# Seven block products in place of eight in part of w_down of a hybrid decoder layer

## The chip, the cores and the metric

The kernel runs on one core of one Trainium2 chip. TensorE (PE) multiplies, VectorE (DVE), ScalarE (ACT) and GpSimd (POOL) work on tiles in SBUF, the first two also read the results of TensorE in PSUM, and SyncE (SP) issues nearly all DMAs. The metric is the device time of one execution in microseconds (us), as a median over runs.

## The reference

One decoder layer in float32 on x of 256 tokens by 2048 columns: attention in two groups of heads, then an MLP with gates. Each of the two is wrapped as x + norm(f(norm(x))). The attention and its projections are not touched by the change; the second half is:

```python
h = rmsnorm(x, pre_ffn_g[l])
u = causal_dwconv(h @ w_up[l], conv_w[l], conv_b[l])
gate, val = jnp.split(u, 2, axis=-1)
y = (jax.nn.gelu(gate, approximate=True) * val) @ w_down[l]
x = x + rmsnorm(y, post_ffn_g[l])
```

w_up is 2048 by 11264, w_down is 5632 by 2048 (44 row blocks of 128). Each weight is read from memory once in a run.

## The kernel before

**Numbers.** A float32 operand is split into a high part (hi, a rounded copy that ScalarE writes) and the rest (lo, a subtraction on VectorE), `w_split` for weights (L106) and `split` for activations (L285). A product is three matmuls, hi by hi, hi by lo and lo by hi (`mm3`, L279).

**Weights.** `w_load` (L69) has SP load a unit of 128 by 1024 numbers (512 KB) into one of five `raw` buffers; `w_split` writes its parts to one of five `whi` and five `wlo` buffers (`w_parts`, `WB`). A raw buffer comes free after the subtraction, a whi or wlo buffer after the last matmul that reads it.

**Order of the work.** TensorE's instructions run in the order in which the code is written. From the first group of the MLP (`order.__exit__`) until the last `manual_schedule` near L1010 the other engines' order is made by a planner, by priority (place in the code) and by when operands and buffers are ready. Buffers of a tag are handed out by it too. Each engine executes its queue in order.

**The MLP.** The 5632 hidden columns are worked in two halves of 22 blocks (`FHALF`). A half has 11 groups of two blocks: TensorE computes 256 columns of gates and 256 of values (`proj_T`), `conv` (L849) adds the two parts of the result (L853, L854), scales (GpSimd, L855) and applies the convolution (ScalarE L857, VectorE L859, L861); gate and value are multiplied (L930) and split into G (hi and lo, both 128-token blocks t side by side).

Then comes w_down for that half: for each block of 512 output columns n, two PSUM banks (t = 0 and 1) take 11 units of two row blocks, 12 matmuls a unit. `down` (L943) takes a bank to y_sb: in half 0 a copy on ScalarE, in half 1 an addition on VectorE, a sum of squares on ScalarE and a multiplication by the norm's gain on GpSimd (L951). In half 1 the last 512 columns go otherwise: rows of t = 0 in `b0`; rows of t = 1 in two banks `b1` of 256 columns each, for the first five units (`LAST`) beside `b0`, for the last six (`HOLD`) after it, from parts that are kept (`held`; two units of them in `rest`). `finish` (L990) multiplies by the norm's factor, adds x_sb and sends the result out.

**Memory.** PSUM has four banks with the tag "acc" and four with "att"; the groups of the up-projection take them in turn (`alt`). x_sb (256 by 2048, tag "x") stays in SBUF from the end of the attention until `finish`.

## Time and profile before

| | us |
|---|---|
| time, median of 3 runs (1067.03 to 1067.55) | 1067.05 |
| profiled execution, its own time | 1067.17 |
| its span, first to last instruction | 1065.3 |
| TensorE's clock in it, as granted | 0.998 |
| up-projection of half 1, stage window 695.80 to 936.70 | 240.9 |
| w_down of half 0, 576.00 to 696.00 | 120.0 |
| w_down of half 1, 936.70 to 1057.30 | 120.6 |
| from there to the end | 8.0 |

The stage windows give, for a stretch of the span, the busy time of each engine with its count of instructions in brackets, then the granted clock, the share of the DMA engines and GB/s. A group of instructions reads: line, engine, operation, tile written<-tiles read, shapes, count, then busy time in us and mean ns of one, then the engine's idle time just before them and which instruction ended it. A timeline reads: start, length, engine, line, operation, count. In all of them matmuls are pipelined, so that the record of one overlaps the next.

### The profile page before, as it was taken

Reading aid. Unit: us, or ns where it says so; the run is one execution under the profiler, and the core shown is the slowest. Engines: PE = TensorE matmul, PEld = TensorE weight load, DVE = VectorE, ACT = ScalarE, POOL = GpSimd, SP = SyncE. Lnnn points to the kernel's source line nnn. Section 1 sums busy time; section 2 is a strip of 40 time slices with the busy share of each in tenths; the row PEclk is TensorE's granted clock in tenths of the full one; section 3 lists DMA queues with packets and bytes.
Section 4 is the critical chain, followed back from the end, with each engine's and each line's share of the span. In section 5 each row is a group of like instructions: output and inputs, shape, how many; then the busy total and the mean of one; then the engine's idle time right before and its main releaser. Section 6 shows DMA issues by size and latency. Waiting matters only on the chain.

```text
span 1065.3 us, 16215 instructions
## 1 busy us (share of the span) xinstructions
PE 1055.4 (99%) x5974; PEld 919.2 (86%) x5974; DVE 738.3 (69%) x1200; ACT 614.0 (58%) x1062; POOL 226.2 (21%) x250
## 2 busy tenths in 40 slices
PE   9999999999999999999999999999999999999997
PEld 7889988888889888888888888888888888888886
DVE  5989868886568877777677444457777777755563
ACT  6776757767548655556565443456565555644450
POOL 4353245440122312112121000002121212201110
PEclk9999999999999999999999999999999999999999
DMA  8645667545863766566666666666666666666642
GB/s 290 191 127 175 181 191 213 176 153 160 296 223 122 236 197 193 183 198 197 197 187 185 202 196 195 194 186 198 183 199 192 195 181 198 197 195 194 192 170 79
DMA packets 164970, 202.88 MB, mean 190 GB/s; under 512 B 6780, under 2 KB 130972, under 8 KB 164380
## 3 DMA queue, kind: packets, MB, share of 16 engines
q1 hardware_dynamic: 164572, 201.45, 61.2%
q8 instruction: 47, 0.77, 0.3%
q10 hardware_dynamic: 320, 0.40, 0.1%
q14 instruction: 31, 0.25, 0.1%
HBM read 199.58 MB, written 2.11 MB: 189 GB/s over the span
## 4 chain that ended last, share of the span: by engine, by line
PE 94%; DVE 2%; issue 1%; DMA 1%; ACT 1%; POOL 1%; SPq 0%; DVEq 0%; POOLq 0%; ACTq 0%
PE bank_acc L283 34%; PE bank_acc L261 22%; PE bank_att L261 14%; PE bank_acc L268 11%; PE bank_att L268 7%; PE bank_att L449 1%; PE bank_att L484 1%; PE bank_att L493 1%; DVE wlo L120 1%; PE bank_acc L879 1%; PE bank_att L283 1%; DMA x_in<-in_x_dram 1%; PE bank_att L495 0%; PE bank_att L732 0%; POOL scr L416 0%
## 5 line engine op out<-in xcount | busy, mean ns | idle before, releaser
L120 DVE TENSOR_TENSOR wlo<-raw,whi 128x1024 fp32r<-128x1024 f32 (+3 forms) x357 | 435.7, 1230 | 239.1 <-ACT whi L117 232.7
L117 ACT CAST whi<-raw 128x1024 fp32r<-128x1024 f32 (+3 forms) x356 | 363.3, 1035 | 269.2 <-issue 121.2
L261 PE MATMUL bank_acc<-hT,whi 128*128 128x512 f32 x1088 | 260.6, 391 | 0.0
L261 PEld LDWEIGHTS bank_acc<-hT,whi 128*128 128x128 f32 x1088 | 200.1, 188 | 39.5
L283 PE MATMUL bank_acc<-whi,G 128*128 128x512 f32 x652 | 202.7, 389 | 0.0
L855 POOL TENSOR_TENSOR u<-u,rowf 128x256 f32<-128x256 f32 x88 | 96.6, 1118 | 493.5 <-DVE u L854 490.6
L261 PE MATMUL bank_att<-hT,whi 128*128 128x512 f32 x640 | 150.6, 390 | 0.0
L283 PEld LDWEIGHTS bank_acc<-whi,G 128*128 128x128 f32 x652 | 122.4, 188 | 25.0
L261 PEld LDWEIGHTS bank_att<-hT,whi 128*128 128x128 f32 x640 | 118.7, 188 | 23.9
L268 PEld LDWEIGHTS bank_acc<-hT,wlo 128*128 128x128 f32 x1088 | 131.1, 188 | 3.3
L268 PE MATMUL bank_acc<-hT,wlo 128*128 128x256 f32 x1088 | 133.4, 278 | 0.0
L283 PE MATMUL bank_acc<-wlo,G 128*128 128x512 f32 x326 | 126.9, 389 | 0.0
L283 PE MATMUL bank_acc<-whi,oT 128*128 128x512 f32 (+1 forms) x272 | 81.7, 379 | 0.0
L268 PEld LDWEIGHTS bank_att<-hT,wlo 128*128 128x128 f32 x640 | 76.0, 188 | 1.7
L268 PE MATMUL bank_att<-hT,wlo 128*128 128x256 f32 x640 | 76.3, 277 | 0.0
L283 PEld LDWEIGHTS bank_acc<-wlo,G 128*128 128x128 f32 x326 | 61.2, 188 | 12.3
L283 PEld LDWEIGHTS bank_acc<-whi,oT 128*128 128x128 f32 x272 | 50.2, 188 | 9.3
L283 PE MATMUL bank_acc<-wlo,oT 128*128 128x512 f32 (+1 forms) x136 | 51.2, 377 | 0.0
L283 PE MATMUL bank_acc<-whi,hT 128*128 128x384 f32 (+1 forms) x192 | 46.9, 323 | 0.0
L857 ACT ACTIVATE yg<-u,cw 128x256 f32<-128x256 f32 x44 | 26.5, 602 | 27.5 <-POOL u L855 27.5
L857 ACT ACTIVATE yv<-u,cw 128x256 f32<-128x256 f32 x44 | 26.4, 603 | 26.5 <-POOL u L855 26.5
L416 POOL TENSOR_TENSOR scr<-scr 128x256 f32<-128x256 f32 x26 | 26.7, 1042 | 57.2 <-DVE scr L415 34.3
(212 smaller groups left out, 1056.5 us busy)
## 6 DMA issues: line engine op xcount, KB each, us to landing
raw<-in_w_up_dram SPq DMA_DIRECT2D x176, 512.0 KB, 4.1
raw<-in_w_down_dram SPq DMA_DIRECT2D x88, 512.0 KB, 4.7
raw<-in_w_in_dram SPq DMA_DIRECT2D x51, 512.0 KB, 4.7
raw<-in_w_out_dram SPq DMA_DIRECT2D x32, 512.0 KB, 4.7
raw<-in_w_in_dram SPq DMA_DIRECT2D x16, 384.0 KB, 3.3
cb<-c_dram SPq DMA_DIRECT2D x8, 256.0 KB, 4.3
x_sb<-in_x_dram SPq DMA_DIRECT2D x2, 1024.0 KB, 5.9
raw<-in_w_in_dram SPq DMA_DIRECT2D x5, 408.0 KB, 4.1
```

Source lines behind the costliest of these rows:

```text
L117: i1 = act.copy(hi[:, cs], raw[:, cs])
L120: i2 = dve.tensor_tensor(lo[:, cs], raw[:, cs], hi[:, cs].bitcast(F32), op=ALU.subtract)
L261: pe.matmul(b, hi[:, a, m * P:(m + 1) * P], hT[:, kt, 0:512], start=(kt == 0), stop=(last == (0, kt)))
L268: pe.matmul(b[:, 256:512], lo[:, a, m * P:(m + 1) * P], hT[:, u * 4 + a, 0:256], start=False, stop=(last == (1, u * 4 + a)))
L283: pe.matmul(b, a, r[:, cols], start=(first and i == 0), stop=(last and i == 2))
L416: pool.tensor_tensor(dst, dst, row, op=ALU.mult)
L449: pe.matmul(sb[e][:, cs], a[r, t * P:(t + 1) * P], b[r, 0:nk], start=(n == 0), stop=(n == 2))
L484: pe.transpose(pb[:, i * P:(i + 1) * P], p[:, e, c:c + P], ident)
L493: pe.matmul(ov, values(hl, 0), p[:, :, 0:256], start=(n == 0), stop=False)
L855: pool.tensor_tensor(u[:, 2:258], u[:, 2:258], rowf, op=ALU.mult)
L857: act.activation(y, u[:, 2:258], AF.Identity, bias=cw[:, 3, ch:ch + 1], scale=cw[:, 2, ch:ch + 1])
L879: pe.matmul(v(b, t), gate[kt][0][:, ms], v(hT[:, kt, 0:512], t), start=(t == 0 and kt == 0), stop=False)
```

## The change

Of the 11 pairs of row blocks of a half, the first five (`WIN`) are multiplied in Strassen's way, in Winograd's form. With A the two blocks of activations of 128 tokens by two row blocks, and B two row blocks by two column blocks of 512 (two loads, `left` and `right`), eight block products become seven. Three of them are over A11, A12 and A22 themselves, one over S1 = A21+A22 (which takes A21's place in G), three over S2, S3 and S4, which are made once in the up-projection by four sums on GpSimd and kept, split, in `sums`. On the side of the weights four sums of 128 by 512 (T1 to T4) are made on GpSimd for each seven, in place in the raw buffers, after B11, B22 and B21 have been split, and then split themselves.

Each pair of column blocks (n, n+1) now takes all eight banks: b, e, g, h collect the four results directly, and a, c, d, f the four products that several results share. `fold` adds these to y_sb after the fifth seven, on VectorE, and in half 1 on GpSimd too. A round is: three products of a seven, one pair of row blocks in the old way for n (`four`) and one for n+1, then the other four products. There are five such rounds and one without a seven. In half 1 the second column pair has no bank h: its old-way products of n+1 come afterwards, for t = 0 in e and for t = 1 as before in `b1`.

`sums` needs the memory of x_sb: x is written to DRAM in the first group and read back near the end (`x_dram`, `x_end`). In half 1 the four gain multiplications of columns 0 to 1023 are collected (`later_on`) and run after the last fold, and the parity of `alt` is turned round.

```diff
+WIN = 5
...
+        x_dram = tc.dram_tile([2 * P, D], F32, name="x_dram")
...
+            if half:
+                sums = main.tile([P, WIN, 768], F32R, tag="x", name="sums")
             for g in range(FHALF // 2):
                 c0 = (half * (FHALF // 2) + g) * 256
-                alt = g % 2
+                alt = (g + half) % 2
...
+                ys = []
                 for m in range(2):
                     y = conv(bv[m], 44 + c0 // P + m, "yv")
                     dve.tensor_tensor(y, y, gates[m], op=ALU.mult)
+                    ys.append(y)
+                if g < WIN:
+                    if half == 0 and g == 0:
+                        for t in range(2):
+                            sp.dma_start(x_dram[t * P:(t + 1) * P, :], x_sb[:, t, :])
+                        sums = main.tile([P, WIN, 768], F32R, tag="x", name="sums")
+                    s = fp.tile([P, 512], F32, tag="s", name="s")
+                    (a11, a21), (a12, a22) = [(y[:, 0:P], y[:, P:256]) for y in ys]
+                    pool.tensor_tensor(s[:, P:256], a11, a21, op=ALU.subtract)
+                    pool.tensor_tensor(a21, a21, a22, op=ALU.add)
+                    pool.tensor_tensor(s[:, 0:P], a21, a11, op=ALU.subtract)
+                    pool.tensor_tensor(s[:, 256:384], a12, s[:, 0:P], op=ALU.subtract)
+                for m, y in enumerate(ys):
                     gt = G[g * 2 + m]
                     split(gt[:, 0:256], gt[:, 256:512], y)
+                if g < WIN:
+                    split(sums[:, g, 0:384], sums[:, g, 384:768], s[:, 0:384])
...
-                b1 = [bank("att"), bank("att")]
-                for b, cs in zip(b1, halves):
-                    pe.matmul(b[:, cs], G[0][:, 0:P], G[0][:, 0:256], start=True, stop=False)
-                    act.copy(b[:, cs], y_sb[:, 1, 1536:2048][:, cs])
-            def down(t, n, b):
+            gains = []
+            def down(t, n, b, gain=None):
                 ys = y_sb[:, t, n * 512:(n + 1) * 512]
-                if half == 0:
-                    act.copy(ys, b)
-                else:
-                    dve.tensor_tensor(ys, b, ys, op=ALU.add)
+                dve.tensor_tensor(ys, b, ys, op=ALU.add)
+                if half:
                     act.activation(junk, ys, AF.Square, scale=D ** -0.5,
                                    accum_out=ysq[t][:, n:n + 1])
-                    pool.tensor_tensor(ys, ys, gbf[:, n * 512:(n + 1) * 512], op=ALU.mult)
+                    (gain or pool.tensor_tensor)(ys, ys, gbf[:, n * 512:(n + 1) * 512], op=ALU.mult)
             LAST = FHALF // 2 - HOLD
-            for n in range(3 + (half == 0)):
-                b2 = [bank(), bank()]
-                for u in range(FHALF // 2):
-                    hi, lo = w_unit(w_rows(w_down, half * FHALF + u * 2, 2, n * 512, 512), 2, 512)
-                    for a in range(2):
-                        k = u * 2 + a
-                        for t in range(2):
-                            mm3(b2[t], G[k], t, hi[:, a, :], lo[:, a, :], slice(0, 512), k == 0,
-                                k == FHALF - 1)
-                for t in range(2):
-                    down(t, n, b2[t])
+            def products(b, held, hi, lo, opened, closes=False):
+                for i, (x, r) in enumerate(((held[0], hi), (held[0], lo), (held[1], hi))):
+                    pe.matmul(b, x, r, start=b not in opened and not i,
+                              stop=closes and i == 2)
+                opened.append(b)
+            def parts_of(k, t):
+                return G[k][:, t * P:(t + 1) * P], G[k][:, 256 + t * P:256 + (t + 1) * P]
+            def split_512(dst, i, src):
+                cs = slice(i * 512, i * 512 + 512)
+                hi, lo = dst[0][:, cs], dst[1][:, cs]
+                split(hi, lo, src)
+                return hi, lo
+            def seven(n, u, banks, opened):
+                b, e, g, a, c, d, f = banks
+                k = half * FHALF + u * 2
+                left, right = [w_load(w_rows(w_down, k, 2, m * 512, 512), 2, 512)[0]
+                               for m in (n, n + 1)]
+                b11, b21, b12, b22 = (x[:, i * 512:i * 512 + 512] for x in (left, right)
+                                      for i in range(2))
+                s2, s3, s4 = [(sums[:, u, i * P:i * P + P], sums[:, u, 384 + i * P:512 + i * P])
+                              for i in range(3)]
+                dst = w_parts(UNIT, held=False)
+                w11 = split_512(dst, 0, b11)
+                w22 = split_512(dst, 1, b22)
+                w21 = split_512(w_parts(UNIT, held=False), 0, b21)
+                pool.tensor_tensor(b11, b12, b11, op=ALU.subtract)
+                pool.tensor_tensor(b12, b22, b12, op=ALU.subtract)
+                pool.tensor_tensor(b22, b22, b11, op=ALU.subtract)
+                pool.tensor_tensor(b21, b21, b22, op=ALU.subtract)
+                last = u == WIN - 1
+                products(a, parts_of(u * 2, 0), *w11, opened, last)
+                products(b, parts_of(u * 2 + 1, 0), *w21, opened)
+                products(e, s4, *w22, opened)
+                def others():
+                    dst = w_parts(UNIT, held=False)
+                    t1 = split_512(dst, 0, b11)
+                    t3 = split_512(dst, 1, b12)
+                    dst = w_parts(UNIT, held=False)
+                    t2 = split_512(dst, 0, b22)
+                    t4 = split_512(dst, 1, b21)
+                    products(d, parts_of(u * 2, 1), *t1, opened, last)
+                    products(f, s3, *t3, opened, last)
+                    products(c, s2, *t2, opened, last)
+                    products(g, parts_of(u * 2 + 1, 1), *t4, opened)
+                return others
+            def four(n, u, pair, opened):
+                hi, lo = w_unit(w_rows(w_down, half * FHALF + u * 2, 2, n * 512, 512), 2, 512)
+                for i in range(2):
+                    for t in range(2):
+                        products(pair[t], parts_of(u * 2 + i, t), hi[:, i, :], lo[:, i, :], opened,
+                                 u == FHALF // 2 - 1 and i == 1)
+            def fold(n, a, c, d, f):
+                y11, y12, y21, y22 = (y_sb[:, t, m * 512:(m + 1) * 512] for t in range(2)
+                                      for m in (n, n + 1))
+                if half == 0:
+                    act.copy(y11, a)
+                    dve.tensor_tensor(y22, c, y11, op=ALU.add)
+                    dve.tensor_tensor(y12, d, y22, op=ALU.add)
+                    dve.tensor_tensor(y21, f, y22, op=ALU.add)
+                    dve.tensor_tensor(y22, d, y21, op=ALU.add)
+                else:
+                    s = fp.tile([P, 512], F32, tag="s", name="s")
+                    act.copy(s, a)
+                    dve.tensor_tensor(y11, a, y11, op=ALU.add)
+                    dve.tensor_tensor(s, c, s, op=ALU.add)
+                    pool.tensor_tensor(y12, y12, s, op=ALU.add)
+                    dve.tensor_tensor(y12, d, y12, op=ALU.add)
+                    dve.tensor_tensor(s, f, s, op=ALU.add)
+                    pool.tensor_tensor(y21, y21, s, op=ALU.add)
+                    dve.tensor_tensor(s, d, s, op=ALU.add)
+                    pool.tensor_tensor(y22, y22, s, op=ALU.add)
+            for n in (0, 2):
+                opened = []
+                tail = half and n
+                shared = [bank("att") for _ in range(4)]
+                b, e, g = [bank() for _ in range(3)]
+                h = None if tail else bank()
+                for i in range(FHALF // 2 - WIN):
+                    others = i < WIN and seven(n, i, (b, e, g, *shared), opened)
+                    four(n, WIN + i, (b, g), opened)
+                    if not tail:
+                        four(n + 1, WIN + i, (e, h), opened)
+                    if others:
+                        others()
+                    if i == WIN - 1:
+                        fold(n, *shared)
+                        for args, kw in gains:
+                            pool.tensor_tensor(*args, **kw)
+                later_on = None if tail else lambda *args, **kw: gains.append((args, kw))
+                for t, x in enumerate((b, g)):
+                    down(t, n, x, later_on)
+                if not tail:
+                    for t, x in enumerate((e, h)):
+                        down(t, n + 1, x, later_on)
...
-        b0 = bank()
         held = []
-        for u in range(FHALF // 2):
+        for u in range(LAST, FHALF // 2):
             hi, lo = w_unit(w_rows(w_down, FHALF + u * 2, 2, 1536, 512), 2, 512,
                             keep=(None, [rest[:, c:c + 2, :].rearrange("p a c -> p (a c)")
                                          for c in (4 * (u - LAST), 4 * (u - LAST) + 2)])
-                            if LAST <= u < FHALF // 2 - 4 else None)
-            for a in range(2):
-                k = u * 2 + a
-                args = (k, hi[:, a, :], lo[:, a, :])
-                held.append(args)
-                mm3(b0, G[k], 0, *args[1:], whole, k == 0, k == FHALF - 1)
-                for h in range(2 if u < LAST else 0):
-                    mm3(b1[h][:, halves[h]], G[k], 1, *args[1:], halves[h], False, False)
+                            if u < FHALF // 2 - 4 else None)
+            for i in range(2):
+                k = u * 2 + i
+                held.append((k, hi[:, i, :], lo[:, i, :]))
+                products(e, parts_of(k, 0), hi[:, i, :], lo[:, i, :], opened, k == FHALF - 1)
+        x_sb = main.tile([P, 2, D], F32, tag="x", name="x_end")
+        for t in range(2):
+            sp.dma_start(x_sb[:, t, :], x_dram[t * P:(t + 1) * P, :])
+        b1 = [bank("att"), bank("att")]
+        for b, cs in zip(b1, halves):
+            pe.matmul(b[:, cs], G[0][:, 0:P], G[0][:, 0:256], start=True, stop=False)
+            act.copy(b[:, cs], y_sb[:, 1, 1536:2048][:, cs])
         ctx.enter_context(tc.manual_schedule(
             engines={mybir.EngineType.Activation, mybir.EngineType.DVE, mybir.EngineType.Pool,
                      mybir.EngineType.SP}))
         v = before_last(0, 3)
-        down(0, 3, b0)
+        down(0, 3, e)
         r = rstd_y(0, 3, v)
         for n in range(4):
             finish(0, slice(n * 512, (n + 1) * 512), r, sp)
-        last = fp.tile([P, 256], F32, tag="last", name="last")
+        last = fp.tile([P, 256], F32, tag="cs", bufs=3, name="last")
         for h in range(2):
             if h:
                 v = before_last(1, 4)
-            for k, hi, lo in held[LAST * 2:]:
+            for k, hi, lo in held:
                 mm3(b1[h][:, halves[h]], G[k], 1, hi, lo, halves[h], False, k == FHALF - 1)
             square(1, 3 + h, b1[h], halves[h])
             if h:
```

## The prediction

> **What bounds the kernel now.** The page comes first: busy time by engine, and the chain of work that ended last.
>
> ```profile
> span 1065.3 us, 16215 instructions
> PE 1055.4 (99%) x5974; PEld 919.2 (86%) x5974; DVE 738.3 (69%) x1200; ACT 614.0 (58%) x1062; POOL 226.2 (21%) x250
> ...
> PE 94%; DVE 2%; issue 1%; DMA 1%; ACT 1%; POOL 1%; SPq 0%; DVEq 0%; POOLq 0%; ACTq 0%
> ```
>
> TensorE is busy 99% and makes 94% of the chain, so fewer matmuls shorten the kernel as long as the other engines go on feeding it. The next views are of w_down alone: two pieces of the chain (start, length, matmuls), the stage windows of its two halves (length, then busy time of PE, PEld, DVE, ACT, POOL, then the clock), and the groups of the first half.
>
> ```profile
> 576.10 119.68 PE bank_acc L283 x528
> ...
> 936.70 90.47 PE bank_acc L283 x399
> ```
>
> ```profile
> 576.00:696.00 120.00, 120.00 (x531) 99.38 (x530) 58.51 (x55) 52.58 (x58) 2.22 (x2) 1.00 0.63 194
> 936.70:1057.30 120.60, 120.60 (x594) 102.30 (x593) 63.84 (x68) 49.75 (x63) 12.63 (x10) 1.00 0.52 167
> ```
>
> ```profile
> L120 DVE TENSOR_TENSOR wlo<-raw,whi 128x1024 fp32r<-128x1024 f32 x45 | 55.2, 1226 | 63.4 <-ACT whi L117 63.4
> L117 ACT CAST whi<-raw 128x1024 fp32r<-128x1024 f32 x44 | 46.4, 1054 | 61.1 <-PE bank_acc L283 60.1 <-issue 1.0
> ```
>
> First, the price of a matmul: 119.68 us for 528 is 0.2267 us each (the 0.389 us of a record overlaps its neighbours). Second, the direction of waiting: ScalarE waits for TensorE to free a whi buffer (60.1 us), so supply is ahead. Third, the reserve: VectorE has 58.5 of 120 us in use and GpSimd 2.2.
>
> **What is removed.** Half 0 now has 528 products of 512 columns. Afterwards each of its two column pairs has five rounds of 21+24 and a last of 24, 249 in all, together 498: 30 fewer, 6.8 us. Half 1 keeps its count of 512-wide ones (396+66 = 462 before; 249+177+36 = 462 after) and loses the 60 half-width matmuls of rows 128 to 255, columns 1536 on, whose pace two lines of the timeline give:
>
> ```profile
> 1031.22 0.28 PE L283 MATMUL bank_att<-whi,G 128*128 128x256 f32 x1
> ...
> 1031.93 0.40 PE L283 MATMUL bank_acc<-whi,G 128*128 128x512 f32 x1
> ```
>
> Six half-width matmuls start from the first line up to the second, in 0.71 us: 0.118 us each, so 60 are 7.1 us. Gain on TensorE: **13.9 us**, if nothing else ends later.
>
> **What is added.** A "seven" brings four GpSimd sums of 128x512 and seven separate splits of 512 columns (ScalarE copy, VectorE subtraction), where two splits of 1024 stood. The nearest rows (GpSimd's with the least, the median and the longest duration in ns):
>
> ```profile
> L951 POOL TENSOR_TENSOR y_sb<-y_sb,gbc_ffn x7: 1287/1448/2266, 968.4 to 1050.3; 128x512 f32<-128x512 f32 x7
> ```
>
> ```profile
> L855 POOL TENSOR_TENSOR u<-u,rowf x88: 632/642/1625, 351.5 to 938.1; 128x256 f32<-128x256 f32 x88
> ```
>
> ```profile
> L120 DVE TENSOR_TENSOR wlo<-raw,whi 128x512 fp32r<-128x512 f32 x2 | 1.4, 688 | 0.3 <-ACT whi L117 0.3
> L117 ACT CAST whi<-raw 128x512 fp32r<-128x512 f32 x1 | 0.6, 619 | 0.2 <-DMA raw<-in_w_in_dram 0.2
> ```
>
> ScalarE is safe: 7x0.62+2x1.05 = 6.4 us in a round of 45 matmuls (10.2 us). VectorE alone would be too: 7x0.69+2x1.23 = 7.3, and GpSimd alone at 4x1.29 to 4x1.45 = 5.2 to 5.8. But they do not run side by side. The timeline where both work, VectorE then GpSimd:
>
> ```profile
> 1026.16 1.28 DVE L948 TENSOR_TENSOR y_sb<-bank_acc,y_sb 128x512 f32<-128x512 f32 x2
> 1027.35 1.22 DVE L120 TENSOR_TENSOR rest<-raw,rest 128x1024 fp32r<-128x1024 f32 x1
> 1028.49 2.32 DVE L120 TENSOR_TENSOR wlo<-raw,whi 128x1024 fp32r<-128x1024 f32 x1
> ...
> 1030.98 2.05 DVE L120 TENSOR_TENSOR wlo<-raw,whi 128x1024 fp32r<-128x1024 f32 x1
> ```
>
> ```profile
> 1028.27 3.68 POOL L951 TENSOR_TENSOR y_sb<-y_sb,gbc_ffn 128x512 f32<-128x512 f32 x2 [26.95 <-ACT junk L949]
> ```
>
> A split of 1.22 us takes 2.32 and 2.05 beside GpSimd: they take turns. From the end of the 1027.35 split (1028.57) to GpSimd's end (1031.95), 3.38 us hold two GpSimd sums and one split; from the end of that split (1030.81) to the end of the next (1033.03), 2.22 us hold one of each. So a sum holds the other engine up for 1.15 us and a 1024 split for about 1.1. A 512 split I take at 0.60, the pace of the pair at 1026.16 (its ends: half of 1.1, or 0.69).
>
> So one shared resource decides. A seven needs 4x1.15+7x0.60 = 8.8 us of it, a split of 1024 1.1. A **full round** (a seven, two pairs in the old way) needs 11.0 us against TensorE's 10.2. A **tail round** (half 1, columns 1024 on, one pair in the old way) needs 9.9 against 33x0.2267 = 7.5.
>
> Work left over at the start of each half also counts: the convolution of the last group runs after TensorE has begun w_down.
>
> ```profile
> L855 POOL TENSOR_TENSOR u<-u,rowf 128x256 f32<-128x256 f32 x2 | 2.2, 1132 | 8.7 <-DVE u L854 8.7
> L859 DVE SCALAR_TENSOR_TENSOR yv<-u,cw,yv 128x256 f32<-128x256 f32 x2 | 1.3, 672 | 0.4 <-ACT yv L857 0.4
> ...
> L861 DVE SCALAR_TENSOR_TENSOR yv<-u,cw,yv 128x256 f32<-128x256 f32 x2 | 0.9, 480 | 0.0
> ...
> L930 DVE TENSOR_TENSOR yv<-yv,yg 128x256 f32<-128x256 f32 x2 | 0.8, 420 | 0.0
> L287 DVE TENSOR_TENSOR G<-yv,G 128x256 fp32r<-128x256 f32 x2 | 0.8, 419 | 0.0
> ```
>
> That is 3.8+2.2, less the part in which one only waits: 5 us. Against it stands what is done beforehand; five whi buffers allow the first seven's three splits, one old split and the four sums: 1.8+1.1+4.6 = 7.5 us.
>
> *Half 0*, up to the last seven's last product (A22 with its last sum): ten sevens and 22 old splits, 88+24.2+5-7.5 = 109.7 us, against 471 matmuls, 106.8 us: TensorE waits **2.9 us**. *Half 1*: 5x11.0+2.2 for the first columns, 5x9.9 for the tail, 3.5 for three folding sums on GpSimd, +5-7.5: 107.7 us, against 249+4x33+30 = 411 matmuls, 93.2 us: **14.5 us**.
>
> The folds' VectorE additions read PSUM (5.4 us at a stage's change, nine at 0.60). I let GpSimd work beside them; if not, up to 5 us more in each half, and at best nothing. These rows favour the first:
>
> ```profile
> 761.92 0.75 DVE L854 TENSOR_TENSOR u<-bank_acc,cs 128x256 f32<-128x256 f32 x2
> ```
>
> ```profile
> 762.41 2.22 POOL L855 TENSOR_TENSOR u<-u,rowf 128x256 f32<-128x256 f32 x2 [8.72 <-DVE u L854]
> ```
>
> The second addition ends at 762.67, 0.26 us into GpSimd's, and is not stretched. [...]
>
> **Edits taken at little or nothing.** Stage changes: all eight banks are now held, so TensorE needs bank e emptied 9 matmuls (2.0 us) after its last product; the addition takes 0.69, behind a stretched split up to 3.0. Two such places, 0 to 1 us each; 1 in all. Turns between queues (copy, subtraction, sum) cost another 0.5 (0 to 6: nothing, or 0.3 in each of 20 sevens). The sums of activations (four of 128x128 on GpSimd and one split of 384, in ten groups) lie in the up-projection, which takes 21.9 us a group:
>
> ```profile
> 695.80:936.70 240.90, 240.90 (x1411) 212.77 (x1411) 175.30 (x254) 138.93 (x217) 46.61 (x42) 1.00 0.63 192
> ```
>
> VectorE and GpSimd have 222 of 240.9 us there, waits for each other included; 4x0.32 (half the 0.64 that an undisturbed 256-wide one takes) plus 0.5 in five groups adds 9. Cover enough, so nothing; without it 1 to 2 us a half. x goes out and back over SP's queue as two transfers each way:
>
> ```profile
> raw<-in_w_down_dram SPq DMA_DIRECT2D x88, 512.0 KB, 4.7
> ...
> x_sb<-in_x_dram SPq DMA_DIRECT2D x2, 1024.0 KB, 5.9
> ```
>
> Out: up to 12 us of transfer in front of weight loads, which five raw buffers (five units of 2.7 us) cover: nothing, at worst 5. Back: issued when the last sums have been read, behind the weight loads; 48 matmuls (10.9 us) then lie ahead of the first use, 5.9 covers it: nothing, at worst 3.
>
> **Sum.** 1067.17 (the profiled execution: span 1065.3 and 1.9 around it; the median of the runs, 1067.05, is the same within 0.1) -13.9+2.9+14.5+1+0.5 = **1072.2, say 1072 us**.
>
> **Rivals.** *TensorE stays the bound* (faster). If a sum held VectorE up for less, or far more were done ahead, only 1 to 2 us of waits would remain: 1055. Against it: three stretched splits in the rows above. The turning point is at 17.4-5 = 12.4 us of waiting fewer; 80 sums at 0.15 less already give all of this, so a sum at 1.0 us decides: 1060 to 1064 lies between. *Poor packing* (slower still). Queues are in order: if VectorE stands at a split whose sum isn't ready while GpSimd stands at a weight not yet split, the shared time is lost; 0.6 us in each of 20 sevens is 12 more, less the slack of the first rounds: 1079 to 1086. *The raw buffers bind.* A seven holds two of five from load to last split. If its successor's load waited for them, a round would be 4.7+8.8+0.6 = 14 us, some 4 over in 16 rounds: 1130. ScalarE's wait for TensorE, not for a DMA, speaks against it. *The change does nothing* (sevens slip behind and neither gain nor loss shows): the same sum as 1067, an accident inside the first case.
>
> **Chances.** Forecast 1072, own range 1066 to 1078: 0.48. TensorE-bound or nearly, 1054 to 1064: 0.26. Poor packing, 1079 to 1088: 0.18. Over 1088: 0.08. The range 1057 to 1087 leaves out about 0.17. About 0.2% is what a measurement here can tell from no change. Faster by more (under 1064.9): 0.26 and a little of the forecast's edge, 0.29; within: 0.14; slower: 0.57.
>
> **What would show it.** Right: in the stage windows VectorE and GpSimd nearly always one or the other busy; splits of 512 with means of 0.9 us or more; TensorE idle under 3 us in half 0 and some 14 in half 1, nearly all in the tail, before the products of summed weights, released by VectorE; 0.2267 us a matmul as before. Wrong: TensorE without idle time (sums cheaper than 1.15), waits for DMA (raw buffers), waits at the stage changes of several us (banks), or an up-projection longer than 240.9 us (x or the activation sums).

## The result and the profile after

The changed kernel takes **1093.47 us** (median of 4 runs, 1093.23 to 1095.38) against 1067.20 (1067.03 to 1067.55) for the kernel before: a ratio of **1.025** (95% interval 1.0232 to 1.0267). That is slower, as forecast, but by 26 us where 5 were forecast, and outside the range of 1057 to 1087. The profiled execution took 1095.38, 1.9 above the median. The accounts below are made between the spans, 1065.3 and 1093.7: 28.4 us.

The page of the changed kernel, its span, the busy time by engine and the chain of work that ended last:

```profile
span 1093.7 us, 16568 instructions
...
PE 1054.8 (96%) x5884; PEld 909.1 (83%) x5884; DVE 869.4 (79%) x1336; ACT 652.7 (60%) x1168; POOL 412.6 (38%) x376
...
PE 76%; DVE 12%; DMA 4%; POOL 3%; issue 3%; ACT 2%; SPq 0%; POOLq 0%; DVEq 0%; ACTq 0%
```

TensorE has 90 matmuls fewer, as counted, and its busy time is nearly the same: 1054.8 us against 1055.4. That isn't work done: some 7.7 us of it are slower steps (below, "The clock"), and the record of a matmul before a gap covers the gap's first 0.16 us (0.389 us for a step of 0.2267). Its share of the chain falls from 94% to 76%, and VectorE has taken 10 of the 18 points. The stage windows say where (length, busy time of PE, PEld, DVE, ACT, POOL, then the clock): w_down of half 0, the up-projection of half 1, and w_down of half 1.

```profile
575.63:699.98 124.35, 116.76 (x499) 94.80 (x498) 108.64 (x116) 67.67 (x101) 67.53 (x39) 0.97 0.62 190
699.98:940.66 240.68, 240.68 (x1409) 212.55 (x1408) 186.06 (x265) 140.49 (x221) 68.53 (x66) 1.00 0.63 191
940.66:1085.76 145.10, 123.77 (x537) 97.08 (x535) 126.18 (x127) 69.25 (x115) 89.20 (x53) 0.95 0.50 163
```

The up-projection is unchanged, and the stretch ahead of w_down too (it starts at 575.63; before, at 576.00), so the sums of activations and x's way out cost nothing. Everything is in w_down. Without waits half 0 would take 119.7-6.8 = 112.9 us and half 1 121.05-7.1 = 114.0 (the lengths before, from the first matmul to the last in the trace, less what fewer matmuls give). It is over by 11.4 and 31.1 us, 42.5 in all; less the 13.9 us gained that leaves 28.6, the difference of the spans within 0.2. The timeline of TensorE splits these 42.5 by place (the parts come to 43.0):

| where TensorE stands | half 0 | half 1 | both |
|---|---|---|---|
| within rounds | 3.2 | 3.0, and 9.9 in the tail | 16.1 |
| change from one pair of column blocks to the next | 8.25 | 9.3 | 17.6 |
| end: last seven to the separate columns | - | 9.3 | 9.3 |

**Rounds.** The shared time is there as forecast. The groups of the split of 512 and of one of the four sums (count, busy time, mean ns):

```profile
L288 DVE TENSOR_TENSOR wlo<-raw,whi 128x512 fp32r<-128x512 f32 x140 | 133.2, 1006 | 7.3 <-ACT whi L287 6.5
...
L1000 POOL TENSOR_TENSOR raw<-raw 128x512 f32<-128x512 f32 x20 | 36.8, 1842 | 72.0 <-DVE wlo L288 56.4
```

A split of 512 takes 1006 ns in the mean, where an undisturbed one took 688; a sum of this line takes 1842 ns, and the other three lines are alike (1673 to 1918). Two timelines of one tail round, GpSimd and then VectorE, show how they interlock:

```profile
1027.43 1.66 POOL L1000 TENSOR_TENSOR raw<-raw 128x512 f32<-128x512 f32 x1 [2.44 <-DVE wlo L288]
1029.17 1.61 POOL L1001 TENSOR_TENSOR raw<-raw 128x512 f32<-128x512 f32 x1
1030.86 2.15 POOL L1002 TENSOR_TENSOR raw<-raw 128x512 f32<-128x512 f32 x1
1033.09 1.63 POOL L1003 TENSOR_TENSOR raw<-raw 128x512 f32<-128x512 f32 x1
```

```profile
1025.46 4.17 DVE L288 TENSOR_TENSOR wlo<-raw,whi 128x512 fp32r<-128x512 f32 x5
1029.56 2.30 DVE L121 TENSOR_TENSOR wlo<-raw,whi 128x1024 fp32r<-128x1024 f32 x1
1031.79 5.88 DVE L288 TENSOR_TENSOR wlo<-raw,whi 128x512 fp32r<-128x512 f32 x6
```

While GpSimd works, from 1027.43 to 1034.72, sums take 1.61 to 2.15 us, and the splits beside them are stretched too: one of 1024 to 2.30 us (1.22 undisturbed). Over the tail's rounds VectorE is busy all the time, its instructions stretched by GpSimd, which works for 29.43 of the 38.83 us, and TensorE waits:

```profile
1013.57:1052.40 38.83, 31.73 (x130) 23.17 (x129) 38.83 (x32) 18.35 (x28) 29.43 (x17) 1.00 0.49 149
```

The timeline of TensorE gives the length of a round, by a wait that comes back in each:

```profile
1029.69 0.50 PE L973 MATMUL bank_acc<-wlo,G 128*128 128x512 f32 x1 [1.06 <-DVE wlo L288]
...
1039.41 0.50 PE L973 MATMUL bank_acc<-wlo,G 128*128 128x512 f32 x1 [1.03 <-DVE wlo L288]
```

That is 9.72 us, where 33 matmuls need 7.48. Counted from start to start, the full rounds of the first pair took 10.2, 10.2, 11.9, 10.9 and 10.9 to 11.1 us in each half, against 10.2 for 45 matmuls. In half 0's second pair TensorE waits in no round: they took 10.2 each, apart from the gap in the first. e3 shows why (below).

**Changes of the column pair, and the end.** The waits of TensorE, summed by what it waited for (total, times, longest):

```profile
PE bank_acc L973 <- DVE y_sb L963: 12.5, 3, 6.5
PE bank_acc L973 <- DVE wlo L121: 9.6, 12, 3.8
```

The first row is what the prediction took at 1 us: TensorE waits for the additions that empty a bank (L963), in two gaps of 5.60 and 6.49 us. The change in half 0, in the timelines of TensorE, ScalarE and VectorE:

```profile
635.75 0.39 PE L973 MATMUL bank_att<-whi,G 128*128 128x512 f32 x1
641.73 0.76 PE L973 MATMUL bank_acc<-whi,G 128*128 128x512 f32 x1 [5.60 <-DVE y_sb L963]
642.29 0.63 PE L973 MATMUL bank_acc<-wlo,G 128*128 128x512 f32 x1
642.72 0.63 PE L973 MATMUL bank_acc<-whi,G 128*128 128x512 f32 x1
```

```profile
633.10 1.14 ACT L287 CAST whi<-raw 128x512 fp32r<-128x512 f32 x2 [3.78 <-DMA raw<-in_w_down_dram]
```

```profile
629.67 0.68 DVE L288 TENSOR_TENSOR wlo<-raw,whi 128x512 fp32r<-128x512 f32 x1
633.75 3.08 DVE L288 TENSOR_TENSOR wlo<-raw,whi 128x512 fp32r<-128x512 f32 x2 [3.40 <-ACT whi L287]
636.76 0.68 DVE L1036 TENSOR_TENSOR y_sb<-bank_att,y_sb 128x512 f32<-128x512 f32 x1
...
638.67 1.72 DVE L121 TENSOR_TENSOR wlo<-raw,whi 128x1024 fp32r<-128x1024 f32 x1
640.31 0.68 DVE L1039 TENSOR_TENSOR y_sb<-bank_att,y_sb 128x512 f32<-128x512 f32 x1
640.91 2.47 DVE L963 TENSOR_TENSOR y_sb<-bank_acc,y_sb 128x512 f32<-128x512 f32 x4
```

VectorE took its queue in order here: the last product for the fold's banks starts at 628.95 (0.39 us), the fold's first addition only at 636.76 (in e3, where it is queued ahead of the two splits, it runs at 630.29). Behind the split of 629.67 come two splits of the next pair's first seven, whose weights have not landed: VectorE is idle for 3.40 us, and the two then take 3.08 us beside GpSimd's first sums. The fold of the pair that is finished stands behind them (three additions, L1036 on, another split of 1.72 us, and the fourth addition, L1039), and only then the emptying of the banks that TensorE needs. TensorE used up its last product at 636.1 and goes on at 641.73. The chain shows why the weights were late: the load was issued when the splits of the last seven's sums had freed a raw buffer.

```profile
623.97 1.87 DVE wlo L288 x2
626.93 6.14 DMA raw<-in_w_down_dram
```

At the end it is the same pattern with GpSimd in it (the chain, late in half 1):

```profile
1062.23 0.70 DVE s L1044
1062.99 2.21 POOL y_sb L1045
...
1066.60 1.28 POOL y_sb L1048
...
1069.19 1.84 DVE wlo L121
1071.08 5.06 PE bank_acc L973 x11
```

The fold of half 1 goes to and fro between VectorE (L1044, L1046, L1047, L1049) and GpSimd (L1045, L1048, L1050), and the subtraction of a kept weight, for which TensorE waits 3.78 us, stands behind it on VectorE.

**The clock.** After these three gaps, and nowhere else in w_down, the matmuls are also slower: steps of 0.43 us (642.29 to 642.72) for 0.2267. Windows ahead of the three spells, and in the last two, with the clock in the third place from the end:

```profile
636.60:640.00 3.40, 0.00 (x0) 0.00 (x0) 3.37 (x5) 1.18 (x3) 2.63 (x2) 1.00 0.00 0
...
1001.80:1005.20 3.40, 0.00 (x0) 0.00 (x0) 1.25 (x1) 0.00 (x0) 3.32 (x3) 1.00 0.27 53
1005.25:1012.00 6.75, 4.18 (x9) 2.91 (x10) 5.60 (x9) 3.75 (x10) 4.54 (x5) 0.50 0.13 49
...
1066.65:1070.05 3.40, 0.65 (x3) 0.19 (x1) 2.61 (x4) 1.45 (x4) 2.60 (x3) 1.00 0.48 198
1070.10:1076.85 6.75, 5.49 (x13) 4.13 (x13) 4.03 (x5) 0.41 (x2) 4.27 (x2) 0.50 0.00 0
```

Each spell lasts 6.8 us at half the clock. From the number of steps in each that took 0.43 in place of 0.2267 us, I estimate that they cost 2.3 to 2.9 us, 7.7 in all. This is contained in the rows of the table for the changes and the end.

### The profile page after: what moved, and what is told of

Read it like the earlier page. It is cut to its first block, busy times and chain, and to the rows that moved or that the text cites. A ratio compares the mean times of both kernels' runs of the same rounds, so it can differ in the third digit from the quotient of the medians.

```text
span 1093.7 us, 16568 instructions
## 1 busy us (share of the span) xinstructions
PE 1054.8 (96%) x5884; PEld 909.1 (83%) x5884; DVE 869.4 (79%) x1336; ACT 652.7 (60%) x1168; POOL 412.6 (38%) x376
## 4 chain that ended last, share of the span: by engine, by line
PE 76%; DVE 12%; DMA 4%; POOL 3%; issue 3%; ACT 2%; SPq 0%; POOLq 0%; DVEq 0%; ACTq 0%
PE bank_acc L262 20%; PE bank_att L262 14%; PE bank_acc L284 12%; PE bank_acc L269 10%; PE bank_att L269 7%; DVE wlo L288 6%; PE bank_acc L973 5%; DVE wlo L121 3%; DMA raw<-in_w_down_dram 3%; PE bank_att L973 1%; PE bank_att L450 1%; PE bank_att L485 1%; PE bank_att L494 1%; ACT whi L118 1%; POOL raw L1000 1%
## 5 line engine op out<-in xcount | busy, mean ns | idle before, releaser
L121 DVE TENSOR_TENSOR wlo<-raw,whi 128x1024 fp32r<-128x1024 f32 (+3 forms) x317 | 407.6, 1301 | 113.3 <-ACT whi L118 108.7
L118 ACT CAST whi<-raw 128x1024 fp32r<-128x1024 f32 (+3 forms) x316 | 320.9, 1031 | 159.6 <-issue 75.0
L262 PE MATMUL bank_att<-hT,whi 128*128 128x512 f32 x704 | 165.7, 390 | 0.0
L973 PE MATMUL bank_acc<-whi,G 128*128 128x512 f32 x432 | 147.2, 399 | 12.1 <-DVE y_sb L963 12.1
L288 DVE TENSOR_TENSOR wlo<-raw,whi 128x512 fp32r<-128x512 f32 x140 | 133.2, 1006 | 7.3 <-ACT whi L287 6.5
L269 PE MATMUL bank_acc<-hT,wlo 128*128 128x256 f32 x1024 | 125.8, 278 | 0.0
L287 ACT CAST whi<-raw 128x512 fp32r<-128x512 f32 x140 | 80.5, 618 | 61.1 <-POOL raw L1003 16.0
L973 PEld LDWEIGHTS bank_acc<-whi,G 128*128 128x128 f32 x432 | 83.7, 194 | 30.1 <-issue 12.9
L973 PE MATMUL bank_acc<-wlo,G 128*128 128x512 f32 x216 | 88.4, 409 | 15.4 <-DVE wlo L121 9.6
L973 PEld LDWEIGHTS bank_acc<-wlo,G 128*128 128x128 f32 x216 | 41.8, 193 | 31.7 <-DVE wlo L121 14.7
L1000 POOL TENSOR_TENSOR raw<-raw 128x512 f32<-128x512 f32 x20 | 36.8, 1842 | 72.0 <-DVE wlo L288 56.4
```

What stands on the lines that cost most here:

```text
L118: i1 = act.copy(hi[:, cs], raw[:, cs])
L121: i2 = dve.tensor_tensor(lo[:, cs], raw[:, cs], hi[:, cs].bitcast(F32), op=ALU.subtract)
L262: pe.matmul(b, hi[:, a, m * P:(m + 1) * P], hT[:, kt, 0:512], start=(kt == 0), stop=(last == (0, kt)))
L269: pe.matmul(b[:, 256:512], lo[:, a, m * P:(m + 1) * P], hT[:, u * 4 + a, 0:256], start=False, stop=(last == (1, u * 4 + a)))
L287: act.copy(hi, src)
L288: dve.tensor_tensor(lo, src, hi.bitcast(F32), op=ALU.subtract)
```

## The experiments

Every diff is against the changed kernel, cut to what matters.

**e1: the four sums of weights on VectorE.** Is it the time that VectorE and GpSimd share, or the raw buffers?

```diff
-                pool.tensor_tensor(b11, b12, b11, op=ALU.subtract)
+                dve.tensor_tensor(b11, b12, b11, op=ALU.subtract)
...
```

> The four sums of weights of each seven run on VectorE in place of GpSimd; nothing else changes. Theory A (GpSimd and VectorE exclude each other, and the sum of both binds the rounds): a full round then needs 11x0.60+2x1.14 = 8.9 us of VectorE against TensorE's 10.2, a tail round 7.7 against 7.5; the short gaps of TensorE inside the rounds (some 12 us in all) go, 512 splits come back from 1.01 us to 0.69 each, and the time is 1081 us if the gaps at the two changes of column pairs stay, near 1065 if they go with the earlier loads. Theory B (a round is bound by raw buffers: weights' last split, load, sum, split): rounds stay near 10.9 and 9.7 us, 1088 to 1094.

1075.65 us (1.0086 of the kernel before, 1.0069 to 1.0102): 17.8 us less for the same arithmetic, written in the same order. The stage windows of half 0, half 1 and four tail rounds, and the split's group:

```profile
575.46:693.61 118.15, 114.01 (x499) 93.18 (x498) 105.25 (x152) 66.86 (x101) 1.69 (x2) 1.00 0.63 199
934.29:1065.50 131.21, 119.69 (x537) 96.86 (x535) 115.18 (x163) 68.82 (x115) 23.73 (x16) 0.97 0.56 177
1004.00:1035.00 31.00, 31.00 (x135) 24.68 (x134) 30.72 (x48) 19.01 (x30) 0.00 (x0) 1.00 0.66 200
```

```profile
L288 DVE TENSOR_TENSOR wlo<-raw,whi 128x512 fp32r<-128x512 f32 x140 | 92.8, 712 | 8.1 <-ACT whi L287 8.0
```

In the tail TensorE is now busy throughout and GpSimd not at all; VectorE, with the sums besides, keeps pace (a round is 7.5 to 7.8 us). The split falls from 1006 to 712 ns. In the rounds, then, it was the shared time; raw buffers are held across the sums as before, and cost nothing there. What is left, gaps of up to 3.6 us at the changes and one of 3.67 at the end, lies outside the rounds.

**e2: no sums of weights.** The weights are multiplied as they are. How much is left when the sums cost nothing at all?

```diff
-                pool.tensor_tensor(b11, b12, b11, op=ALU.subtract)
-                pool.tensor_tensor(b12, b22, b12, op=ALU.subtract)
-                pool.tensor_tensor(b22, b22, b11, op=ALU.subtract)
-                pool.tensor_tensor(b21, b21, b22, op=ALU.subtract)
```

> The four sums of weights of each seven are left out (the weights are split and multiplied as they are), so that GpSimd does nothing in a round. Theory A (shared time): VectorE needs 6.5 us in a full round, TensorE is the bound; only the changes of column pairs and the end could still leave gaps: 1054 to 1066 us, and the difference to the run with the sums on VectorE tells what they cost there. Theory B (raw buffers): rounds of some 4.7+1+2 us fit under TensorE too, so the same; if gaps of 0.5 us and more stay in every round, neither holds.

1064.32 us (0.9973, 0.9961 to 0.9984). Windows of the two halves:

```profile
575.76:689.65 113.89, 113.13 (x499) 93.42 (x498) 84.02 (x117) 66.73 (x101) 1.69 (x2) 1.00 0.67 208
930.33:1055.93 125.60, 117.58 (x537) 95.80 (x535) 92.30 (x127) 68.62 (x115) 22.88 (x16) 0.99 0.57 185
```

Half 0 is within 1 us of its 112.9. Half 1 is 11.6 over its 114.0 with no sum at all; a gap of 3.8 us stands at the end as before. So, of the 13.9 us gained, 11 go even then (1067.24 - 1064.32 = 2.9 are left): this is the price of the changes and the end, mostly in half 1.

The trace shows one thing more, at the change in half 0. VectorE's queue has the same order there as in the changed kernel (two splits that wait for a load, three additions of the fold, a split, the fourth addition, the emptying):

```profile
628.11 1.29 DVE L288 TENSOR_TENSOR wlo<-raw,whi 128x512 fp32r<-128x512 f32 x2 [2.52 <-ACT whi L287]
...
632.98 2.48 DVE L963 TENSOR_TENSOR y_sb<-bank_acc,y_sb 128x512 f32<-128x512 f32 x4
```

Yet TensorE's gap is 0.76 us, where it was 5.60. The two splits start 4.5 us ahead of TensorE's last product of that stretch (632.65), where they started 2.0 us ahead, and take 1.29 us in place of 3.08; the split behind them takes 1.22 in place of 1.72. So the order is dear only where the sums make the load late and stretch the splits. Counted as steps of TensorE beyond 0.2267 us, the change of half 0 costs 1.0 us here, 4.9 in e1 (sums on VectorE) and 8.2 in the changed kernel; that of half 1 2.2 here (and 2.5 more in the first rounds of the tail, beside the four collected multiplications by the gain), 8.3 in e1 and 9.3.

**e3: the fold first.** Was the change in half 0 a matter of order on VectorE? The last addition of the fold is put ahead of the two splits that waited for a load.

```diff
+                with tc.issue_after(folded[0].ins) if n and not u else ExitStack():
+                    w22 = split_512(dst, 1, b22)
+                    w21 = split_512(w_parts(UNIT, held=False), 0, b21)
```

> Order alone: at the change of column pairs VectorE's additions of fold are queued ahead of the splits of B22 and B21 of the next pair's first seven (in the kernel after, they stand behind them, and these wait for a load until 633.1). Theory A (the gap of 5.6 us in half 0 and 6.5 us in half 1 is VectorE's queue order: fold and the emptying of bank b behind a late load): the gaps fall to 0 to 2 us and with them the spells of half clock; 1093.5 less 5 to 12: 1082 to 1088 us. Theory B (the gaps are the shared time of VectorE and GpSimd, and would come back later as waits for the summed weights): within 3 us of 1093.5.

1090.37 us (1.0216, 1.0201 to 1.0231), 3.1 less.

```profile
575.86:695.70 119.84, 115.83 (x499) 92.71 (x498) 112.41 (x114) 67.01 (x101) 70.88 (x39) 1.00 0.63 196
936.38:1081.14 144.76, 124.98 (x537) 98.08 (x535) 125.84 (x127) 69.36 (x115) 89.05 (x53) 0.94 0.51 164
```

In half 0 the gap of 5.60 us becomes two of 0.56 and 0.57, and the half clock is gone: with the sums as they are, the order made the gap. The change costs 1.9 us in place of 8.2, but the half is only 4.5 us shorter, for 2.0 us come back as waits in the second pair: three of its rounds take 10.8 to 10.9 us, where none took over 10.2 in the changed kernel. There the long gap had given VectorE and GpSimd the time to get ahead (e4, whose extra matmuls hold TensorE's own work up for as long, has no such waits either). In half 1 nothing is gained: gaps of 1.58 and 4.48 us stand in place of 6.49, for its fold still waits for GpSimd.

**e4: TensorE kept at work in the gap.** Is the slow stretch a matter of the clock? 24 more matmuls go into an idle bank ahead of the second pair; their result is not used.

```diff
+                if n:
+                    for _ in range(24):
+                        pe.matmul(shared[0], G[0][:, 0:P], G[0][:, 0:512], start=True, stop=True)
```

> 24 extra matmuls of 512 columns into the idle bank a ahead of the second column pair of each half fill most of the gap at the change; their results are overwritten. Theory A (the half clock of 6.8 us after each gap of over 3.5 us is caused by TensorE's idleness and costs 2.5 us in half 0): no spell of half clock at 640 and 1005 us, half 0 shorter by some 2.5 us, in half 1 0 to 2 us since the tail's rounds are bound by VectorE and GpSimd anyway: 1089 to 1091 us. Theory B (the clock has another cause): the spells stay, and the time with them or up by the part of the extra matmuls that reaches past the gap.

1092.74 us (1.0239, 1.0224 to 1.0254). The runs (1091.73 to 1093.92) overlap those of the changed kernel, so the time alone shows no gain. The windows of half 0 and of ten us behind its change:

```profile
575.78:697.18 121.40, 119.55 (x523) 97.61 (x522) 112.20 (x115) 66.89 (x101) 69.88 (x39) 1.00 0.62 193
637.00:647.00 10.00, 10.00 (x46) 8.29 (x45) 10.00 (x15) 3.28 (x6) 1.70 (x2) 1.00 0.41 109
```

Half 0 is 2.95 us shorter with 24 matmuls more, at a full clock; the price of the half clock was estimated at 2.5. This holds for the two traces only: the changed kernel's execution lies 1.9 us above its median, and e4's 1.0 below. At the change in half 1, 0.52 and 1.04 us of gaps remained close behind each other, and 3.4 us at half clock came even so.

**e5: e1 and e3 together.** 

```diff
+                with tc.issue_after(folded[0].ins) if n and not u else ExitStack():
...
+                dve.tensor_tensor(b11, b12, b11, op=ALU.subtract)
...
```

> Sums of weights on VectorE and, at the change of column pairs, fold queued ahead of the splits of B22 and B21. If the two causes add (shared time in the rounds, queue order at the change): half 0, 118.2 us with the sums moved alone, comes to 114 to 116, half 1 stays within 3 us of 131.2; 1071 to 1074 us. If the order no longer matters once GpSimd is out of the rounds: 1075.7 as before.

1078.29 us (1.0091, 1.0067 to 1.0115; 1072.93 in the profiled execution, 1077.96 to 1078.72 in the three others): a miss, and no better than e1. In the trace half 0 is 115.1 us long, as hoped, but half 1 is 131.4: a gap of 5.59 us at its change and 3.66 at the end. Putting the fold first does no good in half 1, whose fold itself waits for GpSimd.

**e6: e5, with half 1's fold on VectorE alone** (eight additions in place of five, none on GpSimd).

```diff
-                    pool.tensor_tensor(y12, y12, s, op=ALU.add)
                     dve.tensor_tensor(y12, d, y12, op=ALU.add)
+                    dve.tensor_tensor(y12, y12, s, op=ALU.add)
...
-                    dve.tensor_tensor(s, d, s, op=ALU.add)
-                    pool.tensor_tensor(y22, y22, s, op=ALU.add)
+                    dve.tensor_tensor(y22, d, y22, op=ALU.add)
+                    folded[0] = dve.tensor_tensor(y22, y22, s, op=ALU.add)
```

> As the run before, and in half 1 fold's three additions that GpSimd made go to VectorE (eight VectorE additions in a row instead of five that wait for GpSimd in turn). Theory A (the gaps at the change in half 1 and before the kept weights near the end, 3.7 us with a spell of half clock after it, are VectorE's queue standing at a sum that GpSimd hasn't made): half 1 loses 4 to 8 us, 1064 to 1069 us. Theory B (the late loads or the gain multiplications hold the kept weights up): within 2 us of the run before.

1072.42 us (1.0041, 1.0025 to 1.0057; ten runs from 1064.93 to 1074.76). Better than e1 by 3 us, and a miss of the 1064 to 1069 expected: half 1 is 129.1 us long, and 4.33 us of gap remain at its change. In the trace this gap ends with the splits at 993.44, which e3's order has put behind the fold's eight additions and which stand behind the emptyings too: the pinned order is now what TensorE waits for. The gap at the end is in pieces of 2.14 us and less.

**e8: only half 1's fold on VectorE**, in the changed kernel as it is, with the sums on GpSimd. (The same lines as in e6, without the rest.)

```diff
-                    pool.tensor_tensor(y21, y21, s, op=ALU.add)
-                    dve.tensor_tensor(s, d, s, op=ALU.add)
-                    pool.tensor_tensor(y22, y22, s, op=ALU.add)
+                    dve.tensor_tensor(y21, y21, s, op=ALU.add)
+                    dve.tensor_tensor(y22, d, y22, op=ALU.add)
+                    dve.tensor_tensor(y22, y22, s, op=ALU.add)
```

> The kernel after, with fold's three GpSimd additions in half 1 on VectorE and nothing else changed: GpSimd still makes the sums of weights. Theory A (turns between VectorE and GpSimd in fold make the 3.8 us gap near the end and part of the 6.5 us at the change): half 1 4 to 9 us shorter, 1084 to 1090 us. Theory B (the gaps come from the shared time alone): within 2 us of 1093.5.

1087.09 us (1.0189, 1.0172 to 1.0206), 6.4 less.

```profile
939.08:1077.50 138.42, 123.52 (x537) 96.47 (x535) 128.77 (x133) 69.35 (x115) 79.78 (x47) 0.96 0.53 171
```

Half 1 is 6.7 us shorter. The gap at its change falls from 6.49 to pieces of 2.14, 0.95 and 1.18, the one at the end from 3.78 to 1.77. So the additions on GpSimd were a good part of the price of both places, though VectorE has three instructions more.

**e7: e6, with the four collected multiplications by the gain queued on GpSimd behind those of columns 1024 to 1535.**

```diff
-                        for args, kw in gains:
-                            pool.tensor_tensor(*args, **kw)
...
+                elif gains:
+                    with tc.issue_after(geared[0].ins):
+                        for i in (0, 2, 1, 3):
+                            pool.tensor_tensor(*gains[i][0], **gains[i][1])
```

> As the run before, and the four collected gain multiplications on GpSimd are queued behind those of columns 1024 to 1535 instead of at the start of the tail, where each holds VectorE up for 1.15 us. Expected 2 to 5 us less in half 1: 1060 to 1066 us, under the time before the change. If the tail has slack for them, the same as the run before.

1068.32 us (1.0012, 0.9995 to 1.0028; ten runs from 1064.54 to 1072.87): no difference from the kernel before can be told, and the median misses the 1060 to 1066 expected. In its trace w_down has 115.6 and 125.8 us, and no gap over 2.0.

**e10 and e11: the work at the end behind the kept weights.** The fold of the tail, its emptyings and the collected gains are queued behind the last subtraction of the kept weights; e10 has the sums on VectorE, e11 on GpSimd, and the rest is the same.

```diff
+        with tc.issue_after(newest[0].ins):
+            fold(2, *shared)
+            for t, x in enumerate((b, g)):
+                down(t, 2, x)
+            for i in (0, 2, 1, 3):
+                pool.tensor_tensor(*gains[i][0], **gains[i][1])
```

> Sums of weights and all of fold on VectorE, fold ahead at the change of pairs; and near the end fold, the emptying of the last banks and the four collected gain multiplications are queued behind the subtractions of the kept weights. Theory (what is left in the run with the late gains, some 9 us between the last seven's summed products and the separate columns' start where TensorE needs 13.6 us, is VectorE's queue order): that stretch falls from 23.4 to 14 to 17 us, half 1 to 117 to 121, the time to 1058 to 1063 us. Rival: VectorE has as much to do there as TensorE (7x1.1+8x0.6+2x0.6 = 13.7 us), so the gap only moves to the start of the separate columns: 1065 to 1069.

> The same queue order as the run before, but the sums of weights on GpSimd, as the change has them. It leaves the shared time of VectorE and GpSimd as the one large loss: rounds of 10.9 and 9.7 us, so half 1 some 10 to 16 us longer than with the sums on VectorE, half 0 1 to 5 us; 1071 to 1080 us. If the shared time only mattered together with the order, it comes within 4 us of the run before.

e10: 1072.30 us (1.0054, 1.0042 to 1.0066), a miss of both ranges: no gain over e6, and 4 us more than e7, whose end it was to shorten. The wait moved, as the rival had it, and grew; of TensorE's waits in e10 the first is

```profile
PE bank_att L285 <- ACT bank_att L1126: 5.2, 1, 5.2
```

at the start of the separate columns: ScalarE fills their banks (L1126) from the fold's last sum, which now comes late. e11: 1085.57 us (1.0172, 1.0158 to 1.0185), over the 1071 to 1080 expected. With the same order, GpSimd's 80 sums cost 13.3 us more than VectorE's (half 0 119.1 against 115.55 us, half 1 139.5 against 129.6 in their traces).

**e9: Strassen's way in half 0 alone.** The sums on VectorE and the fold first, as in e5; half 1 as it was before the change, with x read back at its start.

```diff
-                if g < WIN:
+                if g < WIN and not half:
...
+                x_sb = main.tile([P, 2, D], F32, tag="x", name="x_end")
+                for t in range(2):
+                    sp.dma_start(x_sb[:, t, :], x_dram[t * P:(t + 1) * P, :])
...
-            for n in (0, 2):
+            for n in (() if half else (0, 2)):
...
+        for n in range(3):
...
```

> Seven products only in half 0, with the sums of weights on VectorE and fold ahead at the change of pairs; half 1 works as in the kernel before. If the parts add, half 0 takes 115 to 118 us as in the last three runs and half 1 121: 1062.5 to 1065.5 us, under the time before the change. If reading x back or the other bank parity costs something in half 1, it shows there and the time is 1066 to 1069.

**1063.99 us** (0.9969, 0.9958 to 0.9980; six runs from 1062.72 to 1065.45): 0.3% faster than the kernel before, and clear of the scatter.

```profile
576.34:691.06 114.72, 113.46 (x499) 93.30 (x498) 103.74 (x150) 66.79 (x101) 1.69 (x2) 1.00 0.64 203
931.74:1052.79 121.05, 121.05 (x597) 102.67 (x595) 64.49 (x68) 50.15 (x64) 13.51 (x10) 1.00 0.53 167
```

Half 0 keeps 5.0 of its 6.8 us, and half 1 is as before to the hundredth. Of the 5.0 the median shows 3.2; what takes the rest lies outside w_down (0.4 ahead of it, 0.3 at the end in the trace) and in the other executions, and was not followed.

## Why the prediction was right in direction and wrong in size

By its own steps:

- **What is removed: right.** 90 matmuls fewer, and a step of those that are left takes 0.2267 us outside the spells of half clock. Half 0 of e2 (113.9 us against 112.9 without waits) shows that its 6.8 us are to be had where the sums cost nothing.
- **One shared resource: right; that the sum fits is partly luck.** Full rounds of 11.0 us were forecast, and those in which TensorE waited took 10.9 to 11.9; tail rounds of 9.9, measured 9.72. The waits in rounds were forecast at 2.9 and 14.5 us, 17.4 in all, and were 16.1 (half 0: 3.2; half 1: 12.9). These alone outweigh the 13.9 us gained, so the direction is no accident. But the forecast let half 0's shortage grow over ten sevens. In the run it is all in three rounds of the first pair, and the second pair has none, since the unforeseen gap gave time to get ahead; in e3, with that gap gone, half 0's rounds cost some 5 us. e1, and e10 against e11, show the cause by taking it away. A split of 512 took 1006 ns in the mean beside GpSimd's sums, and 712 without them (e1).
- **The up-projection and x at nothing: right.** 240.68 us against 240.90, and the way out costs no time ahead of w_down. The loads that bring x back took 9.3 us from issue to landing, where 5.9 was taken, and no engine waited for them.
- **"Stage changes: [...] 0 to 1 us each; 1 in all": this step failed.** They took 17.6 us, and the end, where the prediction had no term at all, 9.3. The prediction counted how long TensorE can go on without bank e (9 matmuls, 2.0 us) and took the addition that empties it as ready to run, behind one stretched split at most. It did not write down VectorE's queue at that place. There, in half 0, stood two splits that waited 3.40 us for a load and then took 3.08, and behind them the fold's four additions with a split of 1.72 us among them. e3 took the order away: 6.4 of 8.25 us at the change went with it, 4.5 of them for good. e2 took the sums away and kept the order, and 1.0 us was left: it takes both, a queue with the fold behind the next pair's splits, and sums that make a load late and stretch the splits. In half 1 the fold's turns with GpSimd are a further cause: e8 took them away and 6.7 us with them, at the change and the end together. The prediction had allowed up to 5 us a half for the folds, if additions from PSUM are held up by GpSimd; the actual mechanism is another, that three of the fold's five additions on VectorE wait until GpSimd has done with the last result, in a queue behind which TensorE's own supply stands.
- **The clock: left out.** The prediction expected 0.2267 us throughout. The three gaps, of 5.60, 6.49 and 3.78 us, were paid again in part: some 7.7 us of the 26.9 at the changes and the end are half clock, 2.3 to 2.9 a gap. e4 shows it for one of the three, in one execution.
- **Turns between queues at 0.5: can't be judged.** The small gaps within rounds (up to 1.23 us) cannot be told from the shared time, which has the same releaser.

Of the rivals, poor packing (1079 to 1086) came nearest in time and in kind: the order of in-order queues lost the time, but at two stage changes and the end, not in each of the 20 sevens. The raw buffers (1130) fall with e1 as the bound of the rounds; at the change of half 0 a load did come late since its buffer was freed late. Of the signs that the prediction named for itself, splits of 0.9 us or more and TensorE's waits in the tail released by VectorE came; TensorE idle under 3 us in half 0 did not (11.4 us lost there); and the sign it named as wrong, "waits at the stage changes of several us (banks)", is the one that came.

What stays open: how much of half 1's 9.3 us at the change is due to the sums and how much to the fold. e2 left 2.2 us there and 2.5 in the rounds behind it, with the fold as it was and no sums; e8 left gaps of 4.3 us with the sums on GpSimd, e6 4.33 with them on VectorE and another order. No run without sums has the fold on VectorE alone, and none shows an order that serves both the fold and the next pair's splits in time.

## What to carry to other kernels

Where a trace shows two engines stretching each other's instructions (here a split of 1.22 us took 2.30 beside GpSimd's sums), add their times into one account per round: the length of the tail's rounds worked out so was right here to 2%, and moving the sums from GpSimd to VectorE (e1) gained 17.8 us, though VectorE then had more to do. At a stage change with all PSUM banks in use, write down the queue of the engine that empties them, instruction by instruction, with the time at which each one's inputs are there; an instruction that waits for a load or for another engine stands in front of what is queued behind it (here two splits that waited 3.40 us stood in front of the fold), and a planner's order is no protection. Where a change pays in one stage and loses in another, try it in the one alone: with the sums on VectorE and the fold first, five sevens in each of two column pairs of half 0 were worth 3 us (e9), and with those of half 1 the kernel was 11 us slower than before (e5). And a gap can hide waits behind it: after one is taken away, look for them in the rounds that follow (2.0 us came back so in e3).

## What the runs showed of the hardware that was not expected

In the changed kernel's trace the three spells of half clock in w_down start at 640.00, 1005.22 and 1070.07 us and last 6.83 us each; the differences of their starts, 365.2 and 64.85, are 107 and 19 times half that length. In the 3.4 us ahead of each TensorE did little (0, 0 and 0.65 us of work in the windows above), and the first part of each still has gaps in it. In e8, where VectorE's order in half 0 is the same but the load landed earlier, the gap there was 4.67 us, and the change cost 6.5 us in place of 8.2. Less the gap and the 0.16 us of the record ahead of it, I estimate that 1.7 us of this are slower steps, which is 3.4 us at half the clock, half the length of a spell in the changed kernel. After the gaps of 3.6 and 3.7 us in e1 the spell was 3.4 us as well, and so it was in e4 behind 3.41 us in which TensorE was busy for 1.85, with gaps of 0.52 and 1.04:

```profile
1003.19:1006.60 3.41, 1.85 (x8) 0.93 (x7) 2.63 (x5) 1.61 (x4) 2.26 (x2) 1.00 0.00 0
```

The tail's rounds, busy 31.73 of 38.83 us, kept the full clock with gaps of up to 1.23.

Executions of one kernel can differ: e7's ten runs go from 1064.54 to 1072.87 us, where all runs of the kernel before lie between 1066.80 and 1067.92. What decides this was not tried.
